# A gated MLP kernel on one NeuronCore: VectorE's second-half sum placed ahead of the previous block's second gate product

## The chip, the cores and the metric

The kernel runs on one core of one Trainium2 chip. The metric is the device time of one execution in microseconds (us), as medians of several executions. The kernel before took 313.16 us (median of 4 runs, 312.69 to 313.49). So single runs of one kernel differ by 0.8 us there.

## The reference

```python
# x: 16 x 256 x 512, w1: 512 x 4096, w2: 2048 x 512, all float32
h = x @ w1
gate, value = np.split(h, 2, axis=-1)
h = np.maximum(gate, 0) * value
return (h @ w2).astype(np.float32)
```

## The kernel before

The 4096 rows of x are worked on in 4 stages of 1024 rows. In each stage the first matrix product is done in blocks of 128 hidden columns (16 blocks; in stage 0 the first four are done in another way). A block uses a Strassen-like scheme: seven products P1 to P7, each two 128x512 matmuls, instead of eight. The results are collected in three PSUM tiles X, Y and W. ScalarE and VectorE turn them into the two halves of the gated result g: first half g1 from X, second half g2 from Y.

```python
class Block:                       # cut: constructor, mm() and the PSUM pools' definitions
    def P1(self):
        self.mm("P1", self.X, True)                       # X is one of 3 buffers
        nc.scalar.copy(out=self.Y, in_=self.X)            # Y is one of 3 buffers
    def P5(self):
        self.mm("P5", self.W, True)
        nc.scalar.activation(self.p5, self.W, COPY, scale=GS)
    def P2(self):
        self.mm("P2", self.X, False)
    def P6(self):
        self.mm("P6", self.Y, False)
        nc.scalar.activation(self.u2, self.Y, COPY, scale=-GS)            # "u2"
    def P3(self):
        self.mm("P3", self.W, False)
        nc.vector.scalar_tensor_tensor(out=self.c12, in0=self.W, ..., in1=self.u2, ...)   # "c12", L229
        nc.vector.scalar_tensor_tensor(out=self.g[:, self.jb, :TH], in0=self.X, ..., in1=self.c12, ...)  # "g1", L230
    def P7(self):
        self.mm("P7", self.Y, False)
        nc.vector.scalar_tensor_tensor(out=self.c22, in0=self.Y, ..., in1=self.p5, ...)   # "c22", L235
    def P4(self):
        self.mm("P4", self.Y, False)                      # writes the Y that c22 has read
        nc.vector.scalar_tensor_tensor(out=self.g[:, self.jb, TH:], in0=self.Y, ..., in1=self.c22, ...)  # "g2", L239

SLOT = {"P1": 0, "P5": 1, "P2": 3, "P6": 4, "P3": 5, "P7": 9, "P4": 13}   # PERIOD = 7
```

A block takes seven places on TensorE, and P7 and P4 of a block fall into the next block's seven. So TensorE's order is P1(j), P5(j), P7(j-1), P2(j), P6(j), P3(j), P4(j-1), and VectorE's is c12(j), g1(j), g2(j-1), c22(j). Each engine works through its list in this order; waits come from the data.

After the blocks of a stage, TensorE starts the second matrix product. It needs sums of g (called g_S, S1 to S4). GpSimd makes most of them during the blocks, VectorE the rest at the stage's end:

```python
if n == "P1" and s == 0 and jb in (11, 13, 15):          # stage 0, GpSimd; cut
    for m in ("S1", "S3")[:2 - h // 4]:                  # h = jb - 11
        g_sum(nc.gpsimd, go, m, h, h + 2)
...
if s == 0:                                               # end of stage 0, VectorE
    g_sum(nc.vector, go, "S1", 6, 8)
    ...                                                  # S2, S4, then half of S3
```

Of the kernel before, what the change touches and what calls it, by code (L numbers as in the profile page):

```python
# [26 lines left out]
NHC = 8  # L27


@with_exitstack  # L30
def kernel(ctx: ExitStack, tc: tile.TileContext, x, w1, w2, out):






    nc = tc.nc
    x2 = x.flatten_outer_dims()
    out2 = out.flatten_outer_dims()  # L40
    flagpool = ctx.enter_context(tc.tile_pool(name="flagpool", bufs=1))
    flag = flagpool.tile([1, 1], dt.int32, name="flag")
    with ExitStack() as fast:
        unfit = fast_way(fast, tc, x2, w1, w2, out2, flag)
    with tc.If(unfit > 0, label="general"):
        with ExitStack() as general:
            general_way(general, tc, x2, w1, w2, out2)
# [52 lines left out]
def fast_way(ctx, tc, x2, w1, w2, out2, flag):  # L100

    nc = tc.nc
# [5 lines left out]
    NJ = H // P  # L108
# [46 lines left out]
    def w1_ops(eng, jb, n):  # L155
        for t in TURNS:
            w1_one(eng, jb, n, *t)

    def w1_one(eng, jb, n, m, a, b, o):
        eng.tensor_tensor(W(m, jb, n), W(a, jb, n), W(b, jb, n), op=o)  # L160

    def add_w2(m, v):
        nc.gpsimd.dma_start(out=V[m], in_=V[v], accum_op=ADD)
# [12 lines left out]
    def x_tiles():  # L176
        o = {f"A{h}": xpool.tile([P, 4, TH], F16, name=f"x_A{h}") for h in (1, 2)}
        for h in (1, 2):
            for k in (1, 2):
                o[f"A{h}{k}"] = o[f"A{h}"][:, 2 * k - 2:2 * k]  # L180
        for n in ("S1", "S2", "S3", "S4"):
            o[n] = xpool.tile([P, 2, TH], F16, name=f"x_{n}")
        return o
# [11 lines left out]
    class Block:  # L195
# [40 lines left out]

        def P4(self):
            self.mm("P4", self.Y, False)
            nc.vector.scalar_tensor_tensor(out=self.g[:, self.jb, TH:], in0=self.Y, scalar=0.0,  # L239
                                           in1=self.c22, op0=MAX, op1=MULT)  # L240

# [28 lines left out]
    def g_sum(eng, go, n, h0, h1):  # L270
        for m, i0, i1, op in SUMS:
            if m == n:
                eng.tensor_tensor(go[n][:, h0:h1], go[i0][:, h0:h1], go[i1][:, h0:h1], op=op)  # L273
# [69 lines left out]
    def advance(stream, n):  # L343
        for _ in range(n):
            if stream is None or next(stream, 0) == 0:
                return
# [5 lines left out]
    def fetch_w2(i):  # L352
        ks, n = slice(i // 2 * NHC, i // 2 * NHC + NHC), i % 2
        nc.gpsimd.dma_start(out=w2_h[n][:, ks], in_=w2_v[:, ks, n * HALF:(n + 1) * HALF])

    def cast_x(s):
        nc.gpsimd.dma_start(out=x16[s], in_=x2[s * SET:(s + 1) * SET, :])

    def g_tiles():
        g = gpool.tile([P, NJ, SET], F16, name="g")  # L360
        gs = {n: gpool.tile([P, NHC, TH], F16, name=f"g_{n}") for n in ("S1", "S2", "S3", "S4")}
        return g, g_ops(g, gs)

    g, go = g_tiles()
# [19 lines left out]
    def turn_by_dma(s, o, h):  # L384
        for k in range(2):
            nc.sync.dma_start_transpose(out=o[f"A{h + 1}{k + 1}"], in_=x16[s][h * TH:(h + 1) * TH, k * 256:k * 256 + 256])
# [7 lines left out]
    def fetch_rows(s, q):  # L394
        rows[s, q] = xpool.tile([P, 2, D], F16, name=f"xn{q % 2}")
        nc.sync.dma_start(out=rows[s, q], in_=x16[s][q * 256:(q + 1) * 256].rearrange("(b p) d -> p b d", p=P))
# [50 lines left out]
    def x_sum(o):  # L447
        n, i0, i1, op = sums.pop(0)
        nc.vector.tensor_tensor(o[n], o[i0], o[i1], op=op)
# [61 lines left out]
    BY_DVE = 2  # L511
    for s in range(NS):
        if s:
            g, go = g_tiles()
        first = NPLAIN if s == 0 else 0
        blocks = {jb: Block(xo, g, jb) for jb in range(first, NJ)}
        plan = {jb * PERIOD + at: (jb, n) for jb in blocks for n, at in SLOT.items()}
        last = NJ * PERIOD
        stream = mm2_stream(s, go)
        if s == 0:  # L520
            w1_ops(nc.gpsimd, 4, 2)
            fetch_w2(0)
            fetch_w2(1)
            w1_ops(nc.gpsimd, 6, 2)
            fetch_w2(2)
            fetch_w2(3)
            w1_ops(nc.gpsimd, 8, 2)
            w1_ops(nc.gpsimd, 10, 2)
            for to, v in ((V["T1"], V["B11"]), (v_12, w2_h[1]), (V["T4"], V["B21"])):
                nc.sync.dma_start(out=to, in_=v)  # L530
            for t in TURNS:
                w1_one(nc.gpsimd, 12, 4, *t)
                if t[0] == "T2":
                    add_w2("T1", "B12")
                    add_w2("T3", "B22")
            add_w2("T2", "T1")
            cast_x(1)
        for at in range(first * PERIOD, last + PERIOD):
            if at in plan:
                jb, n = plan[at]  # L540
                if n == "P1" and s and jb in (4, 8):
                    fetch_rows(s, 1 + jb // 4)
                if n == "P1" and s == 0 and jb in (11, 13, 15):
                    h = jb - 11
                    if h == 4:
                        add_w2("T4", "T2")
                    for m in ("S1", "S3")[:2 - h // 4]:
                        g_sum(nc.gpsimd, go, m, h, h + 2)
                getattr(blocks[jb], n)()
                if n == "P5":  # L550
                    for f in LOOKS.get((s, jb), ()):
                        f()
                if n == "P4" and s:
                    if jb < NHC:
                        g_sum(nc.gpsimd, go, "S3", jb, jb + 1)
                        if s == 1 and jb in (1, 4):
                            cast_x(2 + jb // 4)
                    elif jb < NJ - BY_DVE:
                        for m in ("S1", "S2", "S4"):
                            g_sum(nc.gpsimd, go, m, jb - NHC, jb - NHC + 1)  # L560
            elif at >= last:
                advance(stream, 4)
            else:
                advance(prev, 4)
        if s == 0:
            g_sum(nc.vector, go, "S1", 6, 8)
            for m in ("S2", "S4"):
                for h in (0, NHC // 2):
                    g_sum(nc.vector, go, m, h, h + NHC // 2)
            g_sum(nc.vector, go, "S3", NHC // 2, NHC)  # L570
        else:
            for m in ("S1", "S2", "S4"):
                g_sum(nc.vector, go, m, NHC - BY_DVE, NHC)
        done = 20
        if s + 1 < NS:
            xo = x_tiles()
            for h in range(2):
                turn_by_dma(s + 1, xo, h)
            for q in range(2):
                fetch_rows(s + 1, q)  # L580
            advance(stream, 100)
            sums = list(SUMS)
            for _ in SUMS:
                x_sum(xo)
            if s == 0:
                w1_ops(nc.vector, 0, 2)
                w1_ops(nc.vector, 2, 2)
            advance(stream, MM2 - TAIL - 100 - done)
        else:
            advance(stream, MM2)  # L590
        prev = stream
# [29 lines left out]
```

## Time and profile before

| | before |
|---|---|
| median time | 313.16 us |
| span of the profiled run | 312.0 us |
| TensorE busy | 97% of the span |
| VectorE busy | 67% |
| two blocks of seven products (mean of ten blocks, P4 starts 98.32 to 128.73) | 6.082 us |

These are lines of the page of the kernel before: busy times, the chain of waits that ended last, and three of its costliest groups. A group's columns are: line, engine, operation, output<-input, shape, count, then busy us and mean ns of one, then idle time of the engine before them and what ended it.

```profile
span 312.0 us, 5142 instructions
...
PE 302.4 (97%) x1867; PEld 182.0 (58%) x1867; DVE 209.4 (67%) x330; ACT 188.9 (61%) x450; POOL 147.7 (47%) x135
...
PE 91%; DVE 3%; DMA 2%; issue 1%; ACT 1%; SPq 0%; DVEq 0%
...
## 5 line engine op out<-in xcount | busy, mean ns | idle before, releaser
...
L202 PEld LDWEIGHTS <-wt 128*128 128x128 f16 x480 | 46.8, 97 | 56.6 <-issue 4.5
...
L229 DVE SCALAR_TENSOR_TENSOR cc<-W,pu 128x512 f32<-128x512 f32 x60 | 41.5, 692 | 35.3 <-ACT pu L223 34.5
...
L202 PE MATMUL Y<-x_A,wt 128*128 128x512 f16 x120 | 35.5, 377 | 0.2 <-DVE cc L235 0.2
```

The next lines are from the chain of waits in time order: start, us until the next piece, engine and group. A product is one piece.

```profile
106.72 0.43 PE Y L202 x2
107.15 0.43 PE W L202 x2
107.58 0.47 PE Y L202 x2
```

(The chain cuts its pieces at the modelled ends of the products, so a piece starts 0.13 to 0.16 us later than the product's own start in the timeline below.) The first two pieces, P6 and P3, last 0.43 us, as nearly all others do, and the last one, a P4, 0.47 us. It is every second P4 that lasts 0.46 or 0.47 us; those between last 0.44 us. The busy time cannot show this, because a matmul's listed duration (0.38 us for one, 0.59 us for two) is longer than its share of the pipeline. Starts can.

This is the same stretch in the timeline, all engines, rows cut: start, duration, engine, line, operation, and in brackets the idle time before it.

```profile
101.37 0.59 PE L202 MATMUL Y<-x_A,wt 128*128 128x512 f16 x2
...
104.16 0.60 ACT L223 ACTIVATE pu<-Y 128x512 f32<-128x512 f32 x1 [0.25 <-PE Y L202]
...
104.79 0.69 DVE L229 SCALAR_TENSOR_TENSOR cc<-W,pu 128x512 f32<-128x512 f32 x1 [0.44 <-ACT pu L223]
...
105.51 0.69 DVE L230 SCALAR_TENSOR_TENSOR g<-X,cc 128x512 f16<-128x512 f32 x1
...
106.12 0.68 DVE L239 SCALAR_TENSOR_TENSOR g<-Y,cc 128x512 f16<-128x512 f32 x1
...
106.72 0.68 DVE L235 SCALAR_TENSOR_TENSOR cc<-Y,pu 128x512 f32<-128x512 f32 x1
...
107.45 0.59 PE L202 MATMUL Y<-x_A,wt 128*128 128x512 f16 x2
```

c22 lasts from 106.72 to 107.40 and P4 starts at 107.45. Going back from P4: c22, g2, g1 and c12 follow each other without a break, c12 waited for u2, u2 for P6, and P6 stands five products behind the P4 of 101.37. That is a loop over two blocks, and it takes 107.45 - 101.37 = 6.08 us. Six products in a row take 2.59 us in this chain, so fourteen would take 6.04 us.

The last lines are from the end of stage 0, again the timeline.

```profile
64.00 3.02 POOL L273 TENSOR_TENSOR g_S<-g 128x1024 f16<-128x1024 f16 x1
...
65.46 2.12 DVE L273 TENSOR_TENSOR g_S<-g 128x1024 f16<-128x1024 f16 x1
...
69.77 2.35 DVE L273 TENSOR_TENSOR g_S<-g,g_S 128x2048 f16<-128x2048 f16 x2
...
72.17 1.48 PE L284 MATMUL W<-w,g_S 128*128 128x256 f16 x12 [0.35 <-DVE g_S L273]
```

GpSimd's last sum of stage 0 (POOL) runs from 64.00 to 67.02. VectorE's first sum, started at 65.46, takes 2.12 us, against 0.69 to 0.78 us for the same size at the ends of stages 1 to 3. VectorE's third sum ends at 72.12, and TensorE starts behind it at 72.17. Counted from starts, TensorE lost 0.65 us here: the group of 28 matmuls at 64.53 and the 36 behind it need 64 x 0.1092 = 6.99 us and would have been through at 71.52. (0.1092 us a matmul: sixteen take 1.75 us elsewhere in the chain.)

### The profile page before, as it was taken

To read this page: it belongs to the slowest core of one execution; us is meant where nothing else is said; L and a number is where in the kernel's file an instruction comes from. 1 tells how busy PE (TensorE), PEld (TensorE's weight loads), DVE (VectorE), ACT (ScalarE), POOL (GpSimd) and SP (SyncE) were. 2 spreads that over 40 slices of the span, in tenths; PEclk is the share of its full clock that TensorE was granted. 3 is DMA by queue.
4 is the path that set the end of the run, shared out by engine and by line. 5 is a ranking of instruction groups with operands and counts; after the bars stand their busy time and mean duration, and the time that the engine had idled before them with its cause. 6 is when DMAs were issued, how large, how long until landed. Compare 5 with 4: busy or idle time off the path is not lost.

```text
span 312.0 us, 5142 instructions
## 1 busy us (share of the span) xinstructions
PE 302.4 (97%) x1867; PEld 182.0 (58%) x1867; DVE 209.4 (67%) x330; ACT 188.9 (61%) x450; POOL 147.7 (47%) x135
## 2 busy tenths in 40 slices
PE   7799999999999999999999999999999999999993
PEld 3654444488854444468874444458884444448883
DVE  1376888898548888884338888885525888888211
ACT  3347767547667676648847666655857667673230
POOL 5679996950004447990002344994001342997000
PEclk9999999999999999999999999999999999999998
DMA  7999989969324370046220010028311101000113
GB/s 242 194 202 204 218 203 222 202 113 222 119 89 101 70 168 0 3 82 154 103 103 34 34 34 2 0 47 156 139 69 67 34 4 31 0 2 0 69 69 137
DMA packets 33450, 30.74 MB, mean 99 GB/s; under 512 B 13873, under 2 KB 27953, under 8 KB 33201
## 3 DMA queue, kind: packets, MB, share of 16 engines
q0 software_dynamic: 10704, 11.54, 22.9%
q1 hardware_dynamic: 22576, 18.75, 20.7%
q8 instruction: 15, 0.25, 0.3%
q10 hardware_dynamic: 144, 0.13, 0.1%
q14 instruction: 11, 0.08, 0.1%
HBM read 24.12 MB, written 11.53 MB: 114 GB/s over the span
## 4 chain that ended last, share of the span: by engine, by line
PE 91%; DVE 3%; DMA 2%; issue 1%; ACT 1%; SPq 0%; DVEq 0%
PE Y L202 25%; PE X L202 16%; PE W L202 16%; PE Y L284 13%; PE W L284 8%; PE X L284 8%; DMA g<-in_w_dram 2%; PE W L257 2%; PE X L257 2%; DVE g_S L273 1%; DVE g L239 0%; ACT x_A L382 0%; SPq L404 0%; DVE wr L390 0%; DVE cc L229 0%
## 5 line engine op out<-in xcount | busy, mean ns | idle before, releaser
L273 POOL TENSOR_TENSOR g_S<-g 128x512 f16<-128x512 f16 (+1 forms) x47 | 60.6, 1331 | 125.8 <-DVE g L239 123.8
L202 PEld LDWEIGHTS <-wt 128*128 128x128 f16 x480 | 46.8, 97 | 56.6 <-issue 4.5
L202 PE MATMUL X<-x_A,wr 128*128 128x512 f16 x240 | 71.3, 378 | 0.2 <-ACT Y L209 0.2
L202 PE MATMUL Y<-x_S,wt 128*128 128x512 f16 x240 | 71.4, 379 | 0.0
L229 DVE SCALAR_TENSOR_TENSOR cc<-W,pu 128x512 f32<-128x512 f32 x60 | 41.5, 692 | 35.3 <-ACT pu L223 34.5
L202 PEld LDWEIGHTS <-wr 128*128 128x128 f16 x360 | 35.0, 97 | 41.2 <-issue 0.5
L209 ACT COPY Y<-X 128x512 f32<-128x512 f32 x60 | 34.2, 570 | 38.9 <-PE X L202 20.9
L284 PEld LDWEIGHTS <-g_S 128*128 128x128 f16 x512 | 49.9, 98 | 6.6 <-DVE g_S L273 0.9
L223 ACT ACTIVATE pu<-Y 128x512 f32<-128x512 f32 x60 | 35.9, 598 | 14.0 <-PE Y L202 14.0
L230 DVE SCALAR_TENSOR_TENSOR g<-X,cc 128x512 f16<-128x512 f32 x60 | 41.5, 692 | 2.3
L239 DVE SCALAR_TENSOR_TENSOR g<-Y,cc 128x512 f16<-128x512 f32 x60 | 40.9, 682 | 2.8 <-PE Y L202 2.8
L284 PEld LDWEIGHTS <-g 128*128 128x128 f16 x384 | 37.6, 98 | 8.2
L235 DVE SCALAR_TENSOR_TENSOR cc<-Y,pu 128x512 f32<-128x512 f32 x60 | 40.9, 682 | 0.1
L216 ACT ACTIVATE pu<-W 128x512 f32<-128x512 f32 x60 | 36.1, 602 | 0.2 <-DVE g L230 0.2
L202 PE MATMUL Y<-x_A,wt 128*128 128x512 f16 x120 | 35.5, 377 | 0.2 <-DVE cc L235 0.2
L202 PE MATMUL W<-x_S,wr 128*128 128x512 f16 x120 | 35.7, 379 | 0.0
L202 PE MATMUL W<-x_S,wt 128*128 128x512 f16 x120 | 35.7, 379 | 0.0
L284 PE MATMUL X<-w,g 128*128 128x256 f16 x256 | 31.2, 272 | 0.0
L284 PE MATMUL Y<-v,g_S 128*128 128x256 f16 x256 | 30.7, 273 | 0.0
L314 DVE SCALAR_TENSOR_TENSOR o<-W,pv 128x256 f32<-128x256 f32 x16 | 6.8, 424 | 32.9 <-PE W L284 32.9
L273 POOL TENSOR_TENSOR g_S<-g,g_S 128x512 f16<-128x512 f16 x18 | 21.8, 1211 | 1.4
L273 POOL TENSOR_TENSOR g_S<-g_S,g 128x512 f16<-128x512 f16 x18 | 20.8, 1157 | 1.4
(69 smaller groups left out, 293.7 us busy)
## 6 DMA issues: line engine op xcount, KB each, us to landing
out_dram<-o SPq DMA_DIRECT2D x16, 256.0 KB, 2.2
out_dram<-pv SPq DMA_DIRECT2D x15, 256.0 KB, 2.0
x<-in_x_dram POOLq DMA_DIRECT2D x3, 1024.0 KB, 9.8
xn<-x SPq DMA_DIRECT2D x12, 256.0 KB, 3.4
wr<-in_w_dram POOLq DMA_DIRECT2D x4, 512.0 KB, 14.2
w<-in_w_dram POOLq DMA_DIRECT2D x4, 512.0 KB, 11.6
wr<-in_w_dram POOLq DMA_DIRECT2D x6, 256.0 KB, 8.9
g_S<-in_x_dram SPq DMA_DIRECT2D x2, 512.0 KB, 4.8
```

The lines of the kernel that those rows point to most:

```text
L202: nc.tensor.matmul(ps, W(wn, self.jb)[:, b], self.xo[xn][:, b, :], start=fresh and b == 0, stop=b == 1, skip_group_check=True)
L209: nc.scalar.copy(out=self.Y, in_=self.X)
L216: nc.scalar.activation(self.p5, self.W, COPY, scale=GS)
L223: nc.scalar.activation(self.u2, self.Y, COPY, scale=-GS)
L229: nc.vector.scalar_tensor_tensor(out=self.c12, in0=self.W, scalar=GS, in1=self.u2, op0=MULT, op1=ADD)
L230: nc.vector.scalar_tensor_tensor(out=self.g[:, self.jb, :TH], in0=self.X, scalar=0.0, in1=self.c12, op0=MAX, op1=MULT)
L235: nc.vector.scalar_tensor_tensor(out=self.c22, in0=self.Y, scalar=-GS, in1=self.p5, op0=MULT, op1=ADD)
L239: nc.vector.scalar_tensor_tensor(out=self.g[:, self.jb, TH:], in0=self.Y, scalar=0.0, in1=self.c22, op0=MAX, op1=MULT)
L257: nc.tensor.matmul(ps[:, ts], W(name, self.jb)[:, e % 2], a[:, e, ts], start=e == 0, stop=e == 3, skip_group_check=True)
L273: eng.tensor_tensor(go[n][:, h0:h1], go[i0][:, h0:h1], go[i1][:, h0:h1], op=op)
L284: nc.tensor.matmul(ps, go[gn][:, k, b * P:(b + 1) * P], V[vn][:, k, :], start=fresh and k == 0, stop=k == NHC - 1, skip_group_check=True)
L314: nc.vector.scalar_tensor_tensor(out=d["o1"][:, HALF:], in0=d["W"], scalar=1 / GS, in1=d["pu"][:, 1], op0=MULT, op1=ADD)
```

## The change

The intent is to let P4's c22 run before the g2 of the previous block, which nobody is in a hurry for. g2(j-1) is now emitted by a new `finish()`, called after P7(j) has emitted c22(j); for the last block of a stage it is called after P4. GpSimd's sums that depend on g2 move with it in the program.

```diff
         def P4(self):
             self.mm("P4", self.Y, False)
+
+        def finish(self):
             nc.vector.scalar_tensor_tensor(out=self.g[:, self.jb, TH:], in0=self.Y, scalar=0.0,
                                            in1=self.c22, op0=MAX, op1=MULT)
...
-                if n == "P1" and s == 0 and jb in (11, 13, 15):
+                if n == "P2" and s == 0 and jb in (11, 13, 15):
...
                 getattr(blocks[jb], n)()
+                ended = jb - (n == "P7") if n == "P7" or (n, jb) == ("P4", NJ - 1) else -1
+                if ended in blocks:
+                    blocks[ended].finish()
...
-                if n == "P4" and s:
-                    if jb < NHC:
+                if ended >= 0 and s:
+                    if ended < NHC:
...              # the same sums as before, with `ended` for `jb`
```

VectorE's order becomes c12(j), g1(j), c22(j), g2(j-1). No operation is added or taken away.

More of the change, by code (lines that the diff above doesn't have):

```diff
@@ L552, in fast_way @@
                         f()
-                if n == "P4" and s:
-                    if jb < NHC:
-                        g_sum(nc.gpsimd, go, "S3", jb, jb + 1)
-                        if s == 1 and jb in (1, 4):
-                            cast_x(2 + jb // 4)
-                    elif jb < NJ - BY_DVE:
+                if ended >= 0 and s:
+                    if ended < NHC:
+                        g_sum(nc.gpsimd, go, "S3", ended, ended + 1)
+                        if s == 1 and ended in (1, 4):
+                            cast_x(2 + ended // 4)
+                    elif ended < NJ - BY_DVE:
                         for m in ("S1", "S2", "S4"):
-                            g_sum(nc.gpsimd, go, m, jb - NHC, jb - NHC + 1)
+                            g_sum(nc.gpsimd, go, m, ended - NHC, ended - NHC + 1)
             elif at >= last:
```

## The prediction

> **What bounds the kernel.** TensorE. The page gives PE 97% of the span, and the chain of waits is 91% PE. Busy time alone proves little (the Trainium skill, "Perfetto Trace Analysis", Per-instruction lifecycle: a matmul's end is estimated, not observed), so I read starts. In the chain in time order, six products (two 128x512 matmuls each) take 2.59 us: 0.432 us each, 216 ns a matmul. The skill ("TensorE: Matmul & The Clock Gate", "Wait — 56ns, not 53.3ns?") gives 215.7 ns back to back when warm, so the array is full there. But one product in fourteen, a P4 (Y<-x_A), lasts 0.46 to 0.47 us. Two blocks take 6.08 us where 14 x 0.432 is 6.04.
>
> **Why.** P4 of block j-1 writes Y, which VectorE's c22 (L235) must have read. In the timeline P4 starts 0.05 us after c22 ends (101.32 to 101.37, 107.40 to 107.45): no slack. VectorE's order in a block is c12(j), g1(j), g2(j-1), c22(j), starts 0.6 to 0.7 us apart, and c12 waits for ScalarE's u2 (0.42 us idle). That closes a loop over two blocks: P4, five products, u2, four VectorE operations, P4. It runs at 6.08 us and sets the pace by a hair.
>
> **What the change does.** No work is added or removed. The order becomes c12(j), g1(j), c22(j), g2(j-1). With the trace's durations, for the block whose c12 starts at 104.79: g1 ends 106.2, P7 ends 106.28, c22 runs 106.30 to 106.98 instead of 106.72 to 107.40, g2(j-1) 106.90 to 107.58 instead of 106.12 to 106.80. P4 is due at 107.4: 0.4 us of slack. The next c12 is released by u2 at 107.8, after g2. Y of j-1 is freed 0.8 us later; its next user, a ScalarE copy, comes near 108.4. P6 gets a new wait on g2, long satisfied. GpSimd's sums of g start some 0.8 us later; at the ends of stages 1 to 3 they have 4 us to spare (S4 ends 214.04, first needed near 218.7).
>
> **Worth.** Excess of P4 over 0.432 us, summed in the chain: 0.31 us in each of stages 1 to 3, so 0.94 us. Stage 0: about 0.35 us of the same, plus one stall before the P4 at 54.98 (0.35 us: a c12 came 0.3 us late, cause not seen). I expect stage 0's part to be mostly given back at its end: there VectorE's sums of g run until 72.1, TensorE waits for them (0.35 us into 72.17), and the first sum takes 2.12 us, against 0.70 at later ends, while GpSimd's own sum runs to 67.0 on its own schedule. VectorE arriving 0.5 us earlier only overlaps it more. Net there 0 to 0.3 us, or slightly worse.
>
> Sum: 313.25 - 0.94 - 0.1 = 312.2 us, a gain of 0.3%. Range 311.4 to 313.1. Faster by over 2%: 0.01; within 2%: 0.98; slower: 0.01.
>
> **What would show it.** Right: P4 pieces of 0.43 us, a two-block pace of 6.04 to 6.05 us; c22 ending some 0.4 us before P4; GpSimd's sums 0.5 to 0.8 us later within a stage; at the end of stage 0, a longer TensorE wait for g_S than 0.35 us. Wrong: P4 still 0.46 us (then c22 was not the gate), or a new wait of P1 to P7 on g2.
>
> **What would make it wrong.** The 0.04 us may be a cost of P4's weight load or semaphore; then 313.2. Stage 0's end may keep its gain (311.8) or cost more where VectorE and GpSimd overlap (312.8). Repeats of before spread 0.8 us, nearly the effect.

## More of the kernel before

TensorE is busy for 97% and 91% of the last chain is TensorE. The line of P4 (`Y<-x_A,wt`) reports 0.2 us of waiting in all for c22 (`DVE cc L235`), which would make VectorE irrelevant. Two other lines contradict this. The weight loads (PEld) report 4.5 us of idle time that ends with "issue", that is, with no wait the profile can name. (All of it, 27 pieces, stands before weight loads of P4.) And VectorE is idle for 35.3 us before c12, on average 0.59 us in each of 60 blocks, nearly all of it waiting for ScalarE's u2.

## The result, and the profile after

The changed kernel took 311.92 us (median of 4 runs, 311.75 to 312.8) against 313.16 us, 1.24 us less. The ratio is 0.9967, with a 95% interval of 0.9944 to 0.999. A ratio is the mean time of one kernel's runs over that of the other's in the same rounds, so it is not quite the ratio of the medians. Executions over 1.5% slower than the fastest of the same kernel are left out of the means. A second measurement (below, as an experiment's companion) gave 0.9963 (0.9949 to 0.9977). So the gain is real and about 1.1 us, a third of one per cent.

The page of the changed kernel, the same lines:

```profile
span 310.2 us, 5097 instructions
...
PE 301.7 (97%) x1867; PEld 183.0 (59%) x1867; DVE 216.4 (70%) x330; ACT 189.0 (61%) x450; POOL 148.3 (48%) x135
...
PE 92%; DMA 2%; DVE 2%; issue 1%; ACT 1%; SPq 0%; DVEq 0%
...
## 5 line engine op out<-in xcount | busy, mean ns | idle before, releaser
...
L202 PEld LDWEIGHTS <-wt 128*128 128x128 f16 x480 | 46.9, 98 | 55.0 <-issue 0.2
...
L229 DVE SCALAR_TENSOR_TENSOR cc<-W,pu 128x512 f32<-128x512 f32 x60 | 41.5, 692 | 23.8 <-ACT pu L223 23.7
...
L202 PE MATMUL Y<-x_A,wt 128*128 128x512 f16 x120 | 35.7, 379 | 0.0
```

The 0.2 us of P4's wait is gone, but the better sign is the weight loads' "issue" idle time, which fell from 4.5 to 0.2 us. VectorE is idle 23.8 us before c12 instead of 35.3 us: less of its waiting falls in that place, and the span is shorter. (VectorE's busy time rises from 209.4 to 216.4 us with the same 330 instructions, mostly because fewer of their listed durations overlap.)

The chain in time order, again P6, P3 and P4:

```profile
105.84 0.43 PE Y L202 x2
106.27 0.43 PE W L202 x2
106.70 0.43 PE Y L202 x2
```

P4 now lasts 0.43 us like the others. The timeline of the same stretch:

```profile
100.50 0.59 PE L202 MATMUL Y<-x_A,wt 128*128 128x512 f16 x2
...
103.29 0.60 ACT L223 ACTIVATE pu<-Y 128x512 f32<-128x512 f32 x1 [0.25 <-PE Y L202]
...
103.92 0.69 DVE L229 SCALAR_TENSOR_TENSOR cc<-W,pu 128x512 f32<-128x512 f32 x1 [0.20 <-ACT pu L223]
...
104.64 0.69 DVE L230 SCALAR_TENSOR_TENSOR g<-X,cc 128x512 f16<-128x512 f32 x1
...
105.45 0.69 DVE L235 SCALAR_TENSOR_TENSOR cc<-Y,pu 128x512 f32<-128x512 f32 x1
...
106.05 0.68 DVE L241 SCALAR_TENSOR_TENSOR g<-Y,cc 128x512 f16<-128x512 f32 x1
...
106.54 0.59 PE L202 MATMUL Y<-x_A,wt 128*128 128x512 f16 x2
```

c22 follows g1 as soon as P7 has ended, ends at 106.14 and leaves P4 free at 106.54. g2 starts only at 106.05. Two blocks take 6.042 us (ten blocks, P4 starts 100.50 to 130.71).

The end of stage 0:

```profile
63.20 3.02 POOL L275 TENSOR_TENSOR g_S<-g 128x1024 f16<-128x1024 f16 x1
...
64.80 1.97 DVE L275 TENSOR_TENSOR g_S<-g 128x1024 f16<-128x1024 f16 x1
...
68.97 2.35 DVE L275 TENSOR_TENSOR g_S<-g,g_S 128x2048 f16<-128x2048 f16 x2
...
71.37 1.48 PE L286 MATMUL W<-w,g_S 128*128 128x256 f16 x12 [0.34 <-DVE g_S L275]
```

Here the picture is as before, only 0.8 us earlier as a whole: GpSimd's sum ends at 66.22 instead of 67.02, VectorE's chain of sums 0.80 us earlier, and TensorE starts again at 71.37.

Starts of the same product in both traces, taken from the chain in time order, show where the time went:

| product | before | after | difference | won since the row above |
|---|---|---|---|---|
| first P1 of stage 0 | 25.31 | 25.16 | -0.15 | 0.15 (start, not the change) |
| first group of the second product, stage 0 | 61.65 | 60.99 | -0.66 | 0.51 |
| first P1 of stage 1 | 86.75 | 85.96 | -0.79 | 0.13 |
| first group of the second product, stage 1 | 135.41 | 134.33 | -1.08 | 0.29 |
| the same, stage 2 | 208.51 | 207.15 | -1.36 | 0.28 |
| the same, stage 3 | 281.62 | 279.97 | -1.65 | 0.29 |
| last group of the second product, stage 3 | 303.65 | 301.99 | -1.66 | 0.01 |

The blocks of each stage won 0.28 to 0.29 us in stages 1 to 3 and 0.51 us in stage 0. The remaining 0.13 us came at the end of stage 0, and the first 0.15 us before any changed instruction had run. The pair as a whole differs by more than the timed kernels do (spans 312.0 and 310.2 us): the profiled run of the kernel before took 313.77 us, longer than any of its four timed runs. So the size of the gain is taken from the ratios, and the table shows its places.

### The profile page after: what moved, and what is told of

Read it like the earlier page. It is cut to its first block, busy times and chain, and to the rows that moved or that the text cites. A ratio compares the mean times of both kernels' runs of the same rounds, so it can differ in the third digit from the quotient of the medians.

```text
span 310.2 us, 5097 instructions
## 1 busy us (share of the span) xinstructions
PE 301.7 (97%) x1867; PEld 183.0 (59%) x1867; DVE 216.4 (70%) x330; ACT 189.0 (61%) x450; POOL 148.3 (48%) x135
## 4 chain that ended last, share of the span: by engine, by line
PE 92%; DMA 2%; DVE 2%; issue 1%; ACT 1%; SPq 0%; DVEq 0%
PE Y L202 25%; PE X L202 17%; PE W L202 17%; PE Y L286 13%; PE W L286 8%; PE X L286 8%; DMA g<-in_w_dram 2%; PE W L259 2%; PE X L259 2%; DVE g_S L275 1%; ACT x_A L384 0%; SPq L406 0%; DVE wr L392 0%; DVE g L241 0%; DVE x_A L377 0%
## 5 line engine op out<-in xcount | busy, mean ns | idle before, releaser
L229 DVE SCALAR_TENSOR_TENSOR cc<-W,pu 128x512 f32<-128x512 f32 x60 | 41.5, 692 | 23.8 <-ACT pu L223 23.7
```

The costliest lines, as they stand in the source:

```text
L229: nc.vector.scalar_tensor_tensor(out=self.c12, in0=self.W, scalar=GS, in1=self.u2, op0=MULT, op1=ADD)
```

## The experiments

The theory: a loop over two blocks, P4 -> (five products) -> u2 -> c12 -> ... -> c22 -> P4, was 0.04 us longer than TensorE's own 6.04 us. One VectorE operation fewer between c12 and c22 opens it. The rivals: P4 has a fixed cost of its own; or the gain came from side effects of moving g2 (fewer waits listed on ScalarE's p5, which went from three semaphores to one in most blocks; GpSimd's later sums); or added VectorE work costs time wherever it stands.

**g1 last.** The kernel before, with g1 instead of g2 moved behind c22. g2 stands no later than before, and p5's list of waits stays as before.

```diff
 def P3(self):                      # after c12
-    g1
 def P7(self):                      # after c22
+    g1
```

> The kernel before with the other product moved: VectorE's order in a block becomes c12(j), g2(j-1), c22(j), g1(j). g2 stands no later than before, and the semaphore lists of ScalarE's p5 stay those of before (three waits). Theory (a loop over two blocks through u2, the VectorE operations from c12 to c22, and P4; one operation fewer between u2 and c22 opens it): P4 pieces of 0.43 us, two-block pace 6.04 to 6.05, about the same time as the changed kernel, ratio 0.996 to 0.998 of before. Rival (the gain comes from what the lateness of g2 brought: fewer waits on p5, other times of GpSimd's sums): pace stays 6.08, ratio 1.000.

Measured: 313.93 us, ratio 1.0017 (0.9997 to 1.0036). The pace was as the theory said, 6.042 us for two blocks with no longer P4, but the time was not. So half of the expectation failed. The trace shows why, at the end of each stage (timeline, TensorE and VectorE rows):

```profile
209.09 1.04 PE L284 MATMUL X<-w,g 128*128 128x256 f16 x8
...
209.90 0.68 DVE L234 SCALAR_TENSOR_TENSOR g<-X,cc 128x512 f16<-128x512 f32 x1
...
210.64 0.60 PE L284 MATMUL X<-w,g 128*128 128x256 f16 x4 [0.51 <-DVE g L234]
```

The group of 8 matmuls at 209.09 is through at 209.96 (8 x 0.1092), and the next starts at 210.64, behind g1 of block 15 (L234 in this kernel): a pause of 0.68 us. This next group is the start of the third P1 of the second product, which takes the X buffer that block 15's g1 frees. The list of waits names it four times, 2.0 us in all, once for each stage. I had checked the buffers of Y and not that one. What was won in the blocks was lost at the stages' ends.

**g1 last, but not in block 15.** The same, with the last block of each stage in the old order.

> The first experiment (g1 after c22) with the last block of each stage left in the old order, so that its X is freed as early as before. If that experiment's pace gain was eaten by the wait of the second product's third group for the X buffer of block 15 (0.68 us of pause in each of 4 stages), this wait goes, the pace stays 6.04: ratio 0.996 to 0.998, about 312.2 to 312.6. If the loss was elsewhere: stays at 1.0017.

Measured: 312.05 us, ratio 0.9968 (0.9949 to 0.9987), pace 6.042 us; the wait for block 15's g1 is gone. This reaches the gain of the change without moving g2 later and without changing p5's waits, so the rival that names these two side effects falls. A fixed cost of P4 falls too, since the same P4 no longer lasts longer. (Another side effect, at the end of stage 0, turns up below.)

**One idle operation, in the kernel before.** A memset of 128x128 f16 on VectorE after g1, in every block. Nobody reads it.

```diff
     g1
+    nc.vector.memset(pad, 1.0)      # pad: 128 x 128 f16
```

> The kernel before with one idle VectorE operation per block, a memset of 128x128 f16 after g1, whose result nobody reads (wanted: about 0.15 to 0.2 us a block). VectorE has 0.42 us idle in each block. Theory (the loop over two blocks has no slack): its whole length is added to each two-block loop, pace 6.08 + 0.15 to 0.2, that is about 28 times this, 4 to 6 us more: 317 to 319 us. Rival (VectorE's order is off the critical path; P4's extra 0.04 us is a fixed cost of P4): the memset goes into the idle time, 313.2 us, pace 6.08.

Measured: 315.69 us, ratio 1.0074 (1.0051 to 1.0097), that is 2.3 us more (0.0074 x 313.6). Pace 6.166 us, 0.084 us more. The expected 4 to 6 us was too much, because I took the memset's length for its cost. The timeline of this run:

```profile
104.81 0.69 DVE L230 SCALAR_TENSOR_TENSOR cc<-W,pu 128x512 f32<-128x512 f32 x1 [0.44 <-ACT pu L224]
...
106.21 0.17 DVE L233 MEMSET pad<- 128x128 f16 x1
106.29 0.63 DVE L241 SCALAR_TENSOR_TENSOR g<-Y,cc 128x512 f16<-128x512 f32 x1
...
106.83 0.68 DVE L237 SCALAR_TENSOR_TENSOR cc<-Y,pu 128x512 f32<-128x512 f32 x1
...
107.56 0.59 PE L203 MATMUL Y<-x_A,wt 128*128 128x512 f16 x2
```

The memset lasts 0.17 us, but g2 starts 0.08 us after it. From c12 to c22 it is 2.02 us, against 1.93 us before (104.79 to 106.72): 0.09 us more, and the pace rose by just that, although VectorE still had 0.44 us of idle time before this c12. An engine that is idle in every block still set the pace.

**Two idle operations, in the kernel before.**

> The kernel before with two memsets after g1. One memset put c22 only 0.08 us later (it overlaps g2), and the pace rose by just 0.08 us per two blocks. A second one should add its own start-to-start time, about 0.17 us: c12 to c22 2.01 + 0.17 = 2.18 us, pace about 6.33 us, 28 x 0.25 = 7 us over before: about 320.5 us (319 to 321.5). Rival (the cost is VectorE's load, not the loop): with 0.33 us still idle before c12 in the one-memset run, the second memset fits: about 315.7.

Measured: 322.81 us, ratio 1.0315 (1.0293 to 1.0337), 9.9 us more. Pace 6.425 us, 0.343 us more. Lines of VectorE in this run's timeline, with a c12 at 106.05:

```profile
107.44 0.17 DVE L233 MEMSET pad<- 128x128 f16 x1
...
107.70 0.17 DVE L234 MEMSET pad<- 128x128 f16 x1
107.78 0.63 DVE L242 SCALAR_TENSOR_TENSOR g<-Y,cc 128x512 f16<-128x512 f32 x1
...
108.33 0.68 DVE L238 SCALAR_TENSOR_TENSOR cc<-Y,pu 128x512 f32<-128x512 f32 x1
```

The second memset starts 0.26 us after the first (it writes the same tile and is listed with a wait for it), not 0.17 us as I had estimated, so c12 to c22 is 2.28 us, 0.35 us more than before. Again the pace took all of it. 2.3 us / 0.084 us and 9.9 us / 0.343 us are 27 and 29: the cost is the added delay times about 28 loops, out of the 30 pairs of blocks in the four stages. The rival, by which the second memset would have fitted into VectorE's idle time (0.33 us before every other c12 of the one-memset run, 0.44 us before those between), falls.

**One and two idle operations, in the changed kernel.**

> The changed kernel with the same memset after g1. Theory: c22 now ends about 0.35 to 0.4 us before it must, so the memset costs nothing in the pace: 6.04 to 6.05 us, 311.8 to 312.4 us, as the changed kernel. Rival (VectorE's added work costs time wherever it stands): some 4 to 6 us more than the changed kernel.

Measured with one: 312.23 us, ratio 0.9962 (0.9943 to 0.9982), pace 6.042 us.

> The changed kernel with two memsets. In the one-memset run c12 still had 0.20 us idle before it and c22 ended some 0.4 us before P4. A second memset of 0.17 us shifts c22 and g2 by 0.17, inside both: pace stays 6.04, 312.0 to 312.6 us, ratio 0.996 to 0.998. If it has to be more than 0.2 us, VectorE's throughput becomes the limit: some us slower.

Measured with two: 312.56 us, ratio 0.9983 (0.9965 to 1.0001), pace 6.042 us. Work that cost 9.9 us in the old order costs nothing in the pace of the new one. The ratio of the second run is higher than the changed kernel's, by less than its interval. Its trace shows 0.35 us at the first P4 of stage 0 (it starts at 30.52, 0.83 us after P3, against 0.48 us in the changed kernel), and 0.30 us more loss at the end of stage 0, where GpSimd's sum ended at 66.85 in this run. One thing in the expectation was wrong: here too the second memset starts 0.26 us after the first, more than the 0.2 us called the limit, and VectorE has no idle time listed before the steady c12 any more, yet the pace held.

**Another link of the same loop.** The kernel before with VectorE untouched, and P6 one place ahead of P2 on TensorE.

```diff
-SLOT = {"P1": 0, "P5": 1, "P2": 3, "P6": 4, "P3": 5, "P7": 9, "P4": 13}
+SLOT = {"P1": 0, "P5": 1, "P6": 3, "P2": 4, "P3": 5, "P7": 9, "P4": 13}
```

> The kernel before with VectorE untouched; another link of the loop is shortened: P6 one place ahead of P2 on TensorE, so ScalarE's u2 can start 0.43 us sooner and c12 is held by P3 instead, about 0.2 us earlier. Theory: the loop gets about 0.2 us shorter, P4 no longer waits, pace 6.04 to 6.05, 312.0 to 312.4 us. Rival (only the place of c22 against g2 matters, or P4's cost is fixed): pace stays 6.08, 313.2. Known risk: P6 now starts about 0.05 us after ScalarE's copy into Y ends, so it may wait a little there.

Measured: 312.62 us, ratio 0.997 (0.995 to 0.9989), pace 6.044 us. The same gain, with g2 and c22 in their old places. The feared wait of P6 for ScalarE's copy did not appear in the steady blocks. The timeline of this run:

```profile
104.98 0.69 DVE L229 SCALAR_TENSOR_TENSOR cc<-W,pu 128x512 f32<-128x512 f32 x1 [0.34 <-PE W L202]
...
106.91 0.68 DVE L235 SCALAR_TENSOR_TENSOR cc<-Y,pu 128x512 f32<-128x512 f32 x1
...
107.75 0.59 PE L202 MATMUL Y<-x_A,wt 128*128 128x512 f16 x2
```

c12 now waits for P3 and no longer for u2, and c22 ends at 107.59, 0.16 us before P4 starts.

The links of the loop, from one block in the steady part of each trace (starts, us):

| kernel | P4 to u2 | u2 to c12 | c12 to c22 | c22 to P4 if it waits | sum | measured two-block pace |
|---|---|---|---|---|---|---|
| before | 2.79 | 0.63 | 1.93 | 0.73 | 6.08 | 6.082 |
| before, one memset | 2.78 | 0.63 | 2.02 | 0.73 | 6.16 | 6.166 |
| before, two memsets | 2.79 | 0.63 | 2.28 | 0.73 | 6.43 | 6.425 |
| changed | 2.79 | 0.63 | 1.53 | 0.73 | 5.68 | 6.042 |
| changed, two memsets | 2.79 | 0.63 | 1.73 | 0.73 | 5.88 | 6.042 |
| before, P6 first | 2.44 | 0.84 | 1.93 | 0.73 | 5.94 | 6.044 |

Where the sum is above 6.04, it is the pace. Where it is below, TensorE's fourteen products are. (The 0.73 us is measured where P4 waits, and taken over to the three kernels where it does not. With the change alone, and with P6 first, the sum is an upper bound, because c22 or c12 waits for a product there, P7 or P3. With P6 first, one of five neighbouring blocks gives 6.00 instead of 5.94 us.)

**The end of stage 0.** GpSimd's last sum of stage 0 is given to VectorE, which makes four rows of S1 in one operation instead of two.

```diff
-    for m in ("S1", "S3")[:2 - h // 4]:
-        g_sum(nc.gpsimd, go, m, h, h + 2)
+    if h < 4:
+        for m in ("S1", "S3"):
+            g_sum(nc.gpsimd, go, m, h, h + 2)
...
-    g_sum(nc.vector, go, "S1", 6, 8)
+    g_sum(nc.vector, go, "S1", 4, 8)
```

It was run on the changed kernel:

> The changed kernel with GpSimd's last sum of stage 0 (S1 of rows 4 and 5, 3.0 us, ending at 66.2) given to VectorE, which then makes S1 of rows 4 to 7 in one operation after the last g2. Theory of stage 0's end (VectorE's chain of sums, held up by GpSimd's overlapping sum, ends late, and TensorE waits about 0.5 us for S4): VectorE's S1 takes about 1.2 us instead of 1.97 for half as much, the chain ends about 0.7 us earlier, TensorE's wait for g_S goes: 311.3 to 311.8, 0.4 to 0.5 us under the changed kernel, ratio about 0.995 of before. Rival (TensorE's wait there is given by VectorE's own later sums): no change or slower, 0.997 or more.

Measured: 311.37 us, ratio 0.9943 (0.9927 to 0.9959). Then three kernels were run side by side on another chip: the move on the kernel before, the changed kernel, and the changed kernel with the move.

> The kernel before (old order of g2 and c22) with GpSimd's last stage-0 sum given to VectorE, as was done to the changed kernel. If stage 0's end takes back what the change gains in stage 0 unless this sum is moved: moving it alone is worth less than with the change, about 0.4 to 0.6 us (TensorE's wait at the end of stage 0 goes, pace stays 6.08): ratio 0.998 to 0.9987. With both, the sum of the whole loop gain (0.31 x 3 plus 0.35 to 0.5 in stage 0, 1.3 to 1.45 us) should stand between this kernel and the changed one with the same move (0.9943). If the two are independent: the change is worth the same 1.0 us with and without the move.

Measured: 312.88 us, ratio 0.9991 (0.9973 to 1.0008), pace as before. That is less than the expected 0.4 to 0.6 us, and the interval includes no gain at all.

> The changed kernel itself, so that the next and the previous are compared on one chip in the same rounds: ratio 0.9965 to 0.998.

Measured: 311.97 us, ratio 0.9963 (0.9949 to 0.9977).

> The changed kernel with the sum moved, once more beside the two: ratio 0.994 to 0.9955, and 0.4 to 0.8 us under the changed kernel, if the wait at the end of stage 0 is what the move takes away.

Measured: 311.38 us, ratio 0.9943 (0.9927 to 0.9958). The end of stage 0 in this run's timeline:

```profile
64.70 1.23 DVE L275 TENSOR_TENSOR g_S<-g 128x2048 f16<-128x2048 f16 x1
...
68.11 2.35 DVE L275 TENSOR_TENSOR g_S<-g,g_S 128x2048 f16<-128x2048 f16 x2
...
70.32 1.91 PE L286 MATMUL W<-w,g_S 128*128 128x256 f16 x16
```

VectorE's S1, twice the size, takes 1.23 us instead of 1.97 us and the chain of sums ends by 70.46. TensorE goes through its 16 matmuls at 70.32 without a pause. In the three runs with the move, TensorE lost nothing here. This version beats the kernel before in two measurements on two chips, and the changed kernel in the one in which both ran side by side (311.38 against 311.97 us).

In the rounds these three shared, the change is worth 0.9963 without the move (1.16 us) and 0.9943 / 0.9991 = 0.9952 with it (1.5 us). The difference, 0.35 us, points the way the theory says, but it is smaller than these intervals. That the end of stage 0 takes back part of the gain is therefore only indicated by the times; the next two paragraphs give what the traces show.

The traces show what fixes that end. In the ten profiled runs in which GpSimd makes its last sum, it took 3.01 to 3.05 us and ended anywhere from 65.81 to 67.48. VectorE's first sum started at different times, took 0.91 to 2.27 us, and always ended 0.55 to 0.56 us after GpSimd's. So it is GpSimd's end that sets VectorE's chain, not VectorE's arrival. TensorE's loss follows from it: counted from starts, it is the time from the group of 28 to GpSimd's end, less about 1.8 us. It was 0.7 us for 2.48 us (before) and 2.51 us (changed, second run), 0.5 us for 2.34 us (changed), 0.3 us for 2.12 us (before, one memset), 0.1 us for 1.95 us (changed, one memset), and nothing for 1.71 and 1.28 us (before, two memsets; g1 last). So where TensorE waits here, what its blocks won in stage 0 is given back, unless GpSimd ends sooner as well.

GpSimd's end did move with the change, and perhaps not by chance. Near 46 GpSimd has to wait for a DMA copy between tiles (`v<-w`, issued by SyncE near 43). From issue to landing this copy took 5.20 to 6.17 us in the five profiled runs with VectorE's old order, 4.32 to 4.68 us in seven of the eight with g1 or g2 moved, and 5.26 us in the eighth (two memsets). In the six slow cases a 16 KB packet of the page's queue "q8 instruction" started 0.3 us or more after the copy's issue, in the seven fast ones before it or within 0.05 us of it (read from the packed trace). So GpSimd's end seems to move with the order of VectorE's program, a side effect of the change; how one brings the other, no run tells. It can add to or take from the gain of stage 0 alone. The gain in stages 1 to 3 comes from the pace, and the pair without a wait here (the move alone, and the change with the move) differs by 1.5 us in time where the traces of the change show 0.51 + 0.86 = 1.37 us won in the blocks.

## Why the prediction was right

- **TensorE bounds the kernel, and P4 waits for c22.** Right. The pace fell from 6.082 to 6.042 us, as forecast (6.04 to 6.05). The loop was shown by lengthening it (two sizes, each reappearing in the pace), by shortening it at three places (g2, g1, P6), and by the slack left in the changed kernel.
- **The size in stages 1 to 3.** Forecast 0.94 us from the summed excess of P4; the traces show 0.86 us.
- **Slack of 0.4 us.** Right. c22 ended at 106.14 and P4 was due at 106.54: 0.40 us from end to start, of which about 0.05 us is needed to pass it on.
- **GpSimd's sums later by 0.5 to 0.8 us, harmless.** Harmless is right, and the delay was 0.89 us. In stage 2 the last sum ended 6.42 us after the start of the second product's first group, against 5.53 us before (213.57 - 207.15 and 214.04 - 208.51). TensorE did not wait for it.
- **Stage 0.** Gained 0.51 us in the blocks, where the prediction has 0.5 us in one place and two terms that add to 0.70 us in another: the stall of 0.35 us was right, but the rest, forecast at 0.35 us, was 0.16 us. "Mostly given back at its end, by a longer wait than 0.35 us" was wrong for the profiled run: the listed wait was 0.34 us, and counted from starts TensorE lost 0.50 us instead of 0.65 us. The step that failed is that GpSimd's end would stay at 67.0. It came 0.80 us sooner, mostly because a DMA it waits for in stage 0, the copy named above, landed sooner (GpSimd waited 2.36 us for it, against 3.02 us). Had GpSimd ended at 67.02 again, the loss would have been about 1.3 us (an estimate from the relation above: 67.02 - 63.88 - 1.8), and all of stage 0's gain given back. In the second run of the changed kernel it ended at 66.34 and the loss was 0.67 us. The ends of the different runs scatter by more than the gain in question, so one pair of profiles could not have decided this.
- **The sum.** Forecast 312.2 us; measured 311.92 us, with a ratio that corresponds to 1.03 us of gain against the forecast 1.04 us (the medians differ by 1.24 us). That the numbers agree so closely is luck: the interval of the ratio spans 0.3 to 1.8 us, and the point above was wrong in its mechanism for this pair.
- **Left open.** In stage 0 one c12 comes 0.3 us late in both kernels, at the same block (52.31 before, 52.04 after, idle 0.76 and 0.51 us). Before, P4 of that block lost 0.35 us by it; in the changed kernel, nothing. What delays it, no run tells.

## What to carry to other kernels

When an engine runs at full rate with small regular hiccups, list the starts of its instructions over a whole period and compare the period with the sum of the parts; the wait table listed 0.2 us where more than 1 us was lost. Then look for a closed loop through the other engines: an engine with idle time in every period can still set the pace, and what counts is how many of its operations stand between the operand that comes last and the result that is waited for. Before moving an operation later, list every buffer that it frees, also those used beyond the end of the loop; forgetting one cost a second, equally good order its whole gain.

## What the Trainium skill lacked or had wrong

- "TensorE: Matmul & The Clock Gate", "Wait — 56ns, not 53.3ns?": its 215.7 ns for back-to-back matmuls of 512 columns is confirmed; the changed kernel's pace is 6.042 us / 28 = 215.8 ns.
- "Perfetto Trace Analysis", Per-instruction lifecycle: it says that a matmul's end is estimated. It does not say that waits shorter than the overlap then disappear from idle times. Here P4 showed 0.2 us of waiting where the chain's starts show 0.3 us a stage and more in stage 0, and the trace's hint was the weight loads' idle time, 4.5 us against 0.2 us.
- "VectorE: DVE Perf Modes", "The DRAIN you can't avoid": it gives no start-to-start times for mixed operations. Here an operation of 0.69 us is followed after 0.61 us, or after 0.72 us if the next reads its result. A memset of 0.17 us between g1 and g2 delayed c22 by 0.09 us, and a second one that waits for the first by 0.26 us more.
- "SBUF — State Buffer", "Who interferes with whom": it says that a VectorE operation with two SBUF inputs contends with a GpSimd operation that reads SBUF. The traces agree, and add a size: VectorE's sum ended 0.55 to 0.56 us after GpSimd's in ten runs, whatever its start, while GpSimd's stayed at 3.01 to 3.05 us. GpSimd's sums of 128x512 in the blocks kept their 1.15 to 1.16 us beside VectorE's operations that read one input from PSUM. Its last sum of stage 2, beside VectorE's sums, took 1.48 us in the kernel before (212.56 to 214.04), and VectorE's second sum there took 1.52 us against 0.69 us for its third.
